# Sums made ahead for 49 pairs of weight chunks instead of 44 in a hybrid decoder layer

## The chip, the cores and the metric

One core of a Trainium2 chip runs the whole layer. The metric is the device time of one execution in microseconds. Engines are named as the profile names them: PE is TensorE's matmul, PEld its weight load, DVE is VectorE, ACT is ScalarE, POOL is GpSimd, SP the engine that issues most loads.

## The reference

```python
s = concat([meta_tokens, x])                       # 16 + 256 tokens, width 2048
s = s + 0.5 * swiglu(rms_norm(s), ffn1_w_gu, ffn1_w_down)     # inner width 5632
h = rms_norm(s); q, k, v, b, c, u = split(h @ w_in)
y_att, y_conv = diff_attention(q, k, v), b * short_conv(c * u)
s = s + sum(sigmoid(h @ w_gate) * (branches @ w_branch)) @ w_out
s = s + 0.5 * swiglu(rms_norm(s), ffn2_w_gu, ffn2_w_down)
out = rms_norm(s)[16:]
```

`swiglu(h, w_gu, w_down)` is `(silu(h @ gate) * (h @ up)) @ w_down`, where gate and up are the two halves of `w_gu`. All is float32.

## The kernel before

Every operand of a product is split into a high part, the value rounded to the short format that TensorE takes (a cast on ScalarE), and a low part, the rest (a subtraction on VectorE): `wh` and `wl` for weights. A product is three matmuls: high by high, low by high, high by low.

The change is in the second feed-forward network, whose gate and up stage has eleven units, 0 to 10, of 512 columns of gate and the same 512 of up. A unit runs over eight pairs of 128-row chunks of the weights. The activation (256 tokens) is the stationary operand, a weight tile the moving one, 512 columns wide. A pair is a 2 by 2 block matrix (two token blocks by two chunks) times a 2 by 2 block matrix (two chunks by gate and up). It is computed in one of three ways, a letter in the unit's plan:

- D: eight products, from two weight tiles of 1024 columns (`wh` and `wl` of one chunk's gate and up).
- S: seven products, from four tiles (512, 1024, 1024 and 1024 columns). Sums of weight blocks (`t13`, `t24`) are made by VectorE when the pair is reached, and sums of activation blocks (`sp`) are needed besides.
- P: seven products like S, but `t13` and `t24` were made in an earlier stage and are loaded from DRAM (`made`), while three instead of four blocks of the weights are loaded.

Each of eight accumulators (`pg1` to `pg7`, `pgx`) fills one PSUM bank. After the last pair VectorE evicts them (lines 692 to 703), ScalarE applies the silu, VectorE multiplies (line 716, `cup`), and in pair 1 of the next unit (the plan's second entry) TensorE transposes `cup` back (line 729, `mt_ps`), one half of it after each of the pair's first tiles.

Sums of the activation are made by `Mixed.combine`: four 128 by 128 sums, cast and subtracted into a tile `sp`. For the second network they are made for pairs 2, 3, 5, 6 and 7 and kept in the pool `a` for all eleven units. The activation `h3` is eight tiles, one per pair; tiles 4 to 7 lie in wide slots of 1280 columns of which they use 1024.

Making ahead is done by `Making`, during the first network: for each P pair and each half of its columns POOL loads four blocks (`mk`), VectorE adds in three instructions (lines 306 to 308), POOL stores (`made`). A step is due every five chunks of the first network's products (`tick`, `TICKS`). Its buffers are three of the pool `aux` and two of the tag `tt`; `aux` also takes the sums `sp` of the attention stage, made near the end of the first network.

A scheduler fixes the order of each engine's instructions when the program is built, from the order in which they are written and its own estimate of when things are ready; at run time each engine keeps that order. Pieces of work put into `side` are taken up one at a time, once a pair. Weight tiles have three buffers each for `wh` and `wl`, so a cast waits until TensorE has finished with the tile three back; loads run up to two pairs ahead, with four buffers `st`, and SP issues them in its order.

Of the kernel before, what the change touches and what calls it, by code (L numbers as in the profile page):

```python
# [9 lines left out]
F32 = mybir.dt.float32  # L10
# [5 lines left out]
P = 128  # L16
# [4 lines left out]
F = 5632  # L21
DC = D // P
GC = 4
GW = GC * P
# [12 lines left out]
PIECE = 320  # L37
# [10 lines left out]
B_PLAN = ("DDDSDSDS", (1, 2), {(2, 1): 3, (4, 1): 5, (6, 1): 7}, ())  # L48
FFN2_FIRST = ("DDDPDPPP", (1,), {}, ())
FFN2 = ("DDPPDSPP", (1,), {(4, 1): 5}, ())  # L50
OUT_FIRST = ("DDSDSDSD", (1,), {(1, 1): 2, (3, 1): 4, (5, 1): 6}, ())
OUT = ("DDDDSDSD", (), {(3, 1): 4, (5, 1): 6}, ())
DOWN_FIRST = ("DDDDDDSD", (1,), {(5, 1): 6}, ())
# [4 lines left out]
TICKS = 5  # L58
MAKE_AHEAD = 3
MAKE_BUFS = N_AUX + 2  # L60
MADE = [(u, p) for u in range(F // GW) for p, kind in enumerate((FFN2 if u else FFN2_FIRST)[0]) if kind == "P"]


@with_exitstack
def decoder_layer(ctx: ExitStack, tc: tile.TileContext, t, out):
    nc = tc.nc
# [52 lines left out]
    def load_vectors():  # L119
# [7 lines left out]
        out=mask[:, T - P :],  # L127
        in_=mask[:, T - P :],
# [25 lines left out]
    class Act:  # L154


        def __init__(self, name, chunks, width, wide_slots=(), piece=None):
            self.width, self.lead = width, 0 if piece is None else piece - width
            self.tiles = []
            for g in range(chunks // 2):  # L160
                if g in wide_slots:
                    w = piece or width
                    raw = apool.tile([P, 4 * PIECE], F32R, tag="big", bufs=N_BIG, name=f"{name}{g}")
                    self.tiles.append(raw[:, : 4 * w].rearrange("p (c l w) -> p c l w", c=2, l=2))
                else:
                    self.tiles.append(apool.tile([P, 2, 2, width], F32R, tag="act", name=f"{name}{g}"))

# [147 lines left out]

    for n, (u, p) in enumerate(MADE):
        spare.extend(Making(n, u, p, k) for k in range(2))
# [212 lines left out]
    class Mixed:  # L530
# [22 lines left out]
        def combine(self, p, f, pool=None):  # L553
            a11, a12, a21, a22 = (f[:, c, i * P : (i + 1) * P] for i in range(2) for c in range(2))
            q = tmp.tile([P, 4, P], F32, tag="sc", name="sums")
            nc.vector.tensor_sub(q[:, 0, :], a21, a22)
            nc.vector.tensor_sub(q[:, 1, :], q[:, 0, :], a11)
            nc.vector.tensor_sub(q[:, 2, :], a11, a21)
            nc.vector.tensor_add(q[:, 3, :], a12, q[:, 1, :])
            if pool is None:  # L560
                sp = (aux if self.in_aux else apool).tile([P, 4, 2, P], F32R, tag="act", name=f"sp{p}")
            else:
                sp = pool.tile([P, 4, 2, P], F32R, tag="norm", bufs=1, name=f"sp{p}")
            nc.scalar.copy(out=sp[:, :, 0, :], in_=q)
            nc.vector.tensor_sub(sp[:, :, 1, :], q, sp[:, :, 0, :].bitcast(F32))
            self.sums[p] = [[sp[:, k, lo, :] for lo in range(2)] for k in range(4)]
# [142 lines left out]
    def gate_up_mix(plan, a, rtok, w_gu, g, m, gi):  # L709


        def end(gt, up):
            for i in range(2):
                r = rtok[:, i : i + 1]
                nc.scalar.activation(gt[:, i, :], gt[:, i, :], AF.Silu, scale=r)
                nc.vector.scalar_tensor_tensor(
                    out=up[:, i, :], in0=up[:, i, :], scalar=r, in1=gt[:, i, :], op0=ALU.mult, op1=ALU.mult
                )
            for k in range(2):
                later.append(lambda k=k: back(m, 2 * gi + k, up, k))  # L720

        mixed(plan, a, w_gu[g], "pg", end, made[g])

    def back(act, g, mt, k):

        pt = bank("mt_ps")
        for c in range(2):
            for i in range(2):
                nc.tensor.transpose(
                    pt[:, (2 * c + i) * P : (2 * c + i + 1) * P], mt[:, i, (2 * k + c) * P : (2 * k + c + 1) * P], ident  # L730
                )
        tl, f = act.tiles[g], pt.rearrange("p (c t) -> p c t", c=2)
        nc.scalar.copy(out=tl[:, :, 0, :], in_=f)
        nc.vector.tensor_sub(tl[:, :, 1, :], f, tl[:, :, 0, :].bitcast(F32))
# [43 lines left out]
    for half in halves:  # L778
        m = gate_up(h1, half, t["ffn1_w_gu"], norm1, 0, before1 if half is halves[0] else None)
# [313 lines left out]
    h3 = Act("h3", DC, SEQ, range(4, NH))  # L1093
    hn = Mixed(h3, G_FFN2, False)
    rtok3 = const.tile([P, 2], F32, name="rtok3")
    nss = const.tile([P, 2, 4], F32, name="nss")

    def squares(i, u, q):
        sq = wide([P, GW], "nsq")
        nc.scalar.activation(  # L1100
            sq, sT[i][u][:, q * GW : (q + 1) * GW], AF.Square, accum_out=nss[:, i, 2 * u + q : 2 * u + q + 1]
        )
# [73 lines left out]
    def out_done(u):  # L1176
        def f():
            if u == 0:
                side.append(lambda: None)
                for p in (0, 2):  # L1180
                    side.append(lambda p=p: [turned(p), turned(p + 1), squares(0, 0, p // 2), squares(1, 0, p // 2)])
                side.append(lambda: [hn.sum_of_parts(2, tmp), hn.sum_of_parts(3)])
            else:
                side.extend(
                    (
                        lambda: [turned(4), squares(0, 1, 0), squares(1, 1, 0)],
                        lambda: [turned(5), hn.sum_of_parts(5)],
                        lambda: [turned(6), squares(0, 1, 1), hn.sum_of_parts(6)],
                        lambda: [turned(7), squares(1, 1, 1)],
                        lambda: hn.sum_of_parts(7),  # L1190
                        norm_tok,
                    )
                )

        return f

    side.extend([lambda: None] * 2)
    side.append(lambda: mo.sum_of_parts(6))
    add_mix(OUT_FIRST, mo, w_out, 0, 0, 1.0, "", out_done(0))
    add_mix(OUT, mo, w_out, 0, 1, 1.0, "", out_done(1))  # L1200
# [33 lines left out]
    w_gu, w_down, w_last = t["ffn2_w_gu"], t["ffn2_w_down"], t["ffn2_w_down_last"]  # L1234
    thirds = [list(range(0, 4)), list(range(4, 8)), list(range(8, ng))]
    for half in thirds:
        m = Act("m", len(half) * GC, SEQ, range(4))
        for gi, g in enumerate(half):
            gate_up_mix(FFN2 if g else FFN2_FIRST, hn, rtok3, w_gu, g, m, gi)
        final = half is thirds[-1]  # L1240
        if final:
            for q in range(2):
                nc.gpsimd.dma_start(
                    out=gfin[q],
                    in_=t["norm_final"][q * W2 : (q + 1) * W2].rearrange("(o d) -> o d", o=1).to_broadcast([P, W2]),
# [74 lines left out]
def _laid_out(np, inputs):  # L1320
# [8 lines left out]
    for name in ("ffn1_w_gu", "ffn1_w_down"):  # L1329
# [15 lines left out]
            np.stack([_quarter(w[2 * p * P : 2 * (p + 1) * P], u * GW + k * GW // 2, GW // 2) for k in range(2)])  # L1345
            for u, p in MADE
        ]
# [8 lines left out]
def _quarter(rows, c, n):  # L1356

    a, b = rows[:P], rows[P:]
    blocks = [a[:, c : c + n], a[:, F + c : F + c + n], b[:, F + c : F + c + n], b[:, c : c + n]]
    return _stacked(blocks)  # L1360
# [24 lines left out]
```

## Time and profile before

| | |
|---|---|
| median of 3 runs | 2138.35 us (2138.34 to 2138.82) |
| profiled execution | 2138.54 us, span 2136.3 us |
| PE busy | 2125.1 us, 99% of the span |
| DVE, ACT, POOL busy | 1709.7 us (80%), 1121.1 us (52%), 126.7 us (6%) |
| DMA | 533.04 MB, mean 250 GB/s |
| `mk` loads, `made` stores | 88 each, 512 KB |
| `t` loads from `made` | 88, 512 KB |

A row of a timeline gives the start in us from the span's start, the duration, the engine, the line, the operation, what it writes and reads, and in brackets the idle time of the engine before it with what ended it. Starts on one engine can lie closer than durations, since instructions overlap at their ends. In this execution the units' eight pairs begin at 1772.9 us for unit 6; units 0 to 3, 4 to 7 and 8 to 10 are each followed by their part of the product with `w_down`.

### The profile page before, as it was taken

To read this page: it belongs to the slowest core of one execution; us is meant where nothing else is said; L and a number is where in the kernel's file an instruction comes from. 1 tells how busy PE (TensorE), PEld (TensorE's weight loads), DVE (VectorE), ACT (ScalarE), POOL (GpSimd) and SP (SyncE) were. 2 spreads that over 40 slices of the span, in tenths; PEclk is the share of its full clock that TensorE was granted. 3 is DMA by queue.
4 is the path that set the end of the run, shared out by engine and by line. 5 is a ranking of instruction groups with operands and counts; after the bars stand their busy time and mean duration, and the time that the engine had idled before them with its cause. 6 is when DMAs were issued, how large, how long until landed. Compare 5 with 4: busy or idle time off the path is not lost.

```text
span 2136.3 us, 33292 instructions
## 1 busy us (share of the span) xinstructions
PE 2125.1 (99%) x13129; PEld 1919.3 (90%) x13129; DVE 1709.7 (80%) x2343; ACT 1121.1 (52%) x1414; POOL 126.7 (6%) x201
## 2 busy tenths in 40 slices
PE   9999999999999999999999999999999999999998
PEld 9999999999999998899998888888888888888887
DVE  7777676667776668867888888899999889988998
ACT  6444443344443455545545555557665566655665
POOL 0111111111111000000000000000000000000000
PEclk9999999999999999999999999999999999999999
DMA  8888988889898545543455555557875888768863
GB/s 302 319 314 318 330 320 315 318 317 329 298 338 314 189 178 187 188 158 140 158 184 191 197 197 196 208 207 251 275 281 202 276 281 290 247 220 298 293 217 138
DMA packets 98364, 533.04 MB, mean 250 GB/s; under 512 B 11680, under 2 KB 11936, under 8 KB 56224
## 3 DMA queue, kind: packets, MB, share of 16 engines
q1 hardware_dynamic: 69696, 432.72, 57.4%
q0 software_dynamic: 27936, 97.53, 13.1%
q8 instruction: 102, 1.67, 0.3%
q10 hardware_dynamic: 576, 0.67, 0.1%
q14 instruction: 54, 0.44, 0.1%
HBM read 478.45 MB, written 48.23 MB: 247 GB/s over the span
## 4 chain that ended last, share of the span: by engine, by line
PE 98%; DVE 1%; ACT 0%; DMA 0%; issue 0%; SPq 0%; DVEq 0%; ACTq 0%
PE pg L595 6%; PE pg L593 6%; PE pg L594 6%; PE pd L397 4%; PE pd L395 4%; PE pu L397 4%; PE pu L395 4%; PE pu L396 4%; PE pd L396 4%; PE pg L397 4%; PE pg L395 4%; PE pg L396 4%; PE pd L595 4%; PE pd L593 4%; PE pd L594 3%; PE g L595 2%
## 5 line engine op out<-in xcount | busy, mean ns | idle before, releaser
L384 DVE TENSOR_TENSOR wl<-st,wh 128x1024 fp32r<-128x1024 f32 (+1 forms) x329 | 400.8, 1220 | 253.2 <-ACT wh L379 253.0
L379 ACT CAST wh<-st 128x1024 fp32r<-128x1024 f32 (+1 forms) x328 | 343.4, 1048 | 484.3 <-PE pd L396 145.4
L499 DVE TENSOR_TENSOR wl<-st,wh 128x1024 fp32r<-128x1024 f32 (+1 forms) x424 | 463.5, 1105 | 55.7 <-ACT wh L498 50.7
L498 ACT CAST wh<-st 128x1024 fp32r<-128x1024 f32 (+1 forms) x424 | 396.5, 959 | 201.1 <-PE pdx L594 59.9
L498 ACT CAST wh<-t 128x1024 fp32r<-128x1024 f32 x182 | 189.5, 1052 | 219.6 <-DVE t L634 148.6
L499 DVE TENSOR_TENSOR wl<-t,wh 128x1024 fp32r<-128x1024 f32 x182 | 220.1, 1223 | 66.7 <-ACT wh L498 63.2
L395 PE MATMUL pg<-h,wh 128*128 128x272 f32 x704 | 201.9, 288 | 1.4 <-ACT h L211 1.4
L397 PE MATMUL pd<-mh,wl 128*128 128x272 f32 x704 | 203.3, 289 | 0.0
L395 PE MATMUL pd<-mh,wh 128*128 128x272 f32 x704 | 202.5, 288 | 0.0
L395 PE MATMUL pu<-h,wh 128*128 128x272 f32 x704 | 202.1, 287 | 0.0
L397 PE MATMUL pu<-h,wl 128*128 128x272 f32 x704 | 202.0, 287 | 0.0
L396 PE MATMUL pu<-h,wh 128*128 128x272 f32 x704 | 201.9, 287 | 0.0
L396 PE MATMUL pg<-h,wh 128*128 128x272 f32 x704 | 201.8, 288 | 0.0
L396 PE MATMUL pd<-ml,wh 128*128 128x272 f32 x704 | 200.9, 285 | 0.0
L397 PE MATMUL pg<-h,wl 128*128 128x272 f32 x704 | 200.2, 288 | 0.1
L593 PE MATMUL pg<-wh,h 128*128 128x512 f32 x366 | 143.5, 392 | 0.0
L594 PE MATMUL pg<-wh,h 128*128 128x512 f32 x366 | 142.8, 390 | 0.0
L595 PE MATMUL pg<-wl,h 128*128 128x512 f32 x366 | 142.4, 392 | 0.0
L395 PEld LDWEIGHTS pg<-h,wh 128*128 128x128 f32 x704 | 133.2, 190 | 1.7 <-ACT h L211 1.7
L396 PEld LDWEIGHTS pd<-ml,wh 128*128 128x128 f32 x704 | 133.6, 190 | 0.0
L396 PEld LDWEIGHTS pg<-h,wh 128*128 128x128 f32 x704 | 133.3, 190 | 0.0
L395 PEld LDWEIGHTS pu<-h,wh 128*128 128x128 f32 x704 | 132.8, 189 | 0.0
(383 smaller groups left out, 4984.2 us busy)
## 6 DMA issues: line engine op xcount, KB each, us to landing
st<-in_ffn_w_gu_dram SPq DMA_DIRECT2D x128, 1024.0 KB, 7.2
st<-in_ffn_w_down_dram SPq DMA_DIRECT2D x82, 1024.0 KB, 5.3
mk<-in_ffn_made_of_dram POOLq DMA_DIRECT2D x88, 512.0 KB, 8.5
made<-mk POOLq DMA_DIRECT2D x88, 512.0 KB, 7.0
t<-made SPq DMA_DIRECT2D x88, 512.0 KB, 5.6
st<-in_ffn_w_gu_dram SPq DMA_DIRECT2D x44, 768.0 KB, 5.8
st<-in_w_in_dram SPq DMA_DIRECT2D x32, 1024.0 KB, 4.8
st<-in_w_gate_dram SPq DMA_DIRECT2D x32, 1024.0 KB, 4.8
```

Of the source, the lines that this page charges most:

```text
L379: nc.scalar.copy(out=wh[:, :m, :], in_=sw)
L384: last_wl[:] = [nc.vector.tensor_sub(wl[:, :m, :], sw, wh[:, :m, :].bitcast(F32)).ins]
L395: nc.tensor.matmul(a, wh[:, i, f], act.part(c, 0, t0, t1), start=first, stop=False)
L396: nc.tensor.matmul(a, wh[:, i, f], act.part(c, 1, t0, t1), start=False, stop=False)
L397: nc.tensor.matmul(a, wl[:, i, f], act.part(c, 0, t0, t1), start=False, stop=last)
L498: part_last[:] = [nc.scalar.copy(out=wh, in_=src).ins]
L499: part_last.append(nc.vector.tensor_sub(wl, src, wh.bitcast(F32)).ins)
L593: nc.tensor.matmul(ps[k], hi, wh, start=first, stop=False)
L594: nc.tensor.matmul(ps[k], lo, wh, start=False, stop=False)
L595: nc.tensor.matmul(ps[k], hi, wl, start=False, stop=left[k] == 0)
```

## The change

Pair 1 of units 6 to 10 becomes a P pair. Its activation sums are made once, by one more entry of `side` in unit 0, and written not into a tile of a pool but into the unused 256 columns of the four wide tiles of `h3`, 128 of high part and 128 of low part in each. That makes their cast and subtraction four instructions of 128 columns each instead of one of 512. The number of P pairs goes from 44 to 49, and with it the halves that are made from 88 to 98.

```diff
+FFN2_MORE = ("DPPPDSPP", (1,), {(4, 1): 5}, ())
...
-MADE = [(u, p) for u in range(F // GW) for p, kind in enumerate((FFN2 if u else FFN2_FIRST)[0]) if kind == "P"]
+MORE_IN = (6, 7, 8, 9, 10)
+def _unit_plan(u):
+    return FFN2_MORE if u in MORE_IN else FFN2 if u else FFN2_FIRST
+MADE = [(u, p) for u in range(F // GW) for p, kind in enumerate(_unit_plan(u)[0]) if kind == "P"]
...
                     raw = apool.tile([P, 4 * PIECE], F32R, tag="big", bufs=N_BIG, name=f"{name}{g}")
                     self.tiles.append(raw[:, : 4 * w].rearrange("p (c l w) -> p c l w", c=2, l=2))
+                    self.rest.append(raw[:, 4 * w : 4 * PIECE])
...
             nc.vector.tensor_add(q[:, 3, :], a12, q[:, 1, :])
+            if pool is self.act:
+                self.sums[p] = []
+                for k in range(4):
+                    sp = self.act.rest[k][:, : 2 * P].rearrange("p (l t) -> p l t", l=2)
+                    nc.scalar.copy(out=sp[:, 0, :], in_=q[:, k, :])
+                    nc.vector.tensor_sub(sp[:, 1, :], q[:, k, :], sp[:, 0, :].bitcast(F32))
+                    self.sums[p].append([sp[:, lo, :] for lo in range(2)])
+                return
...
                         norm_tok,
+                        lambda: hn.sum_of_parts(1, h3),
...
-            gate_up_mix(FFN2 if g else FFN2_FIRST, hn, rtok3, w_gu, g, m, gi)
+            gate_up_mix(_unit_plan(g), hn, rtok3, w_gu, g, m, gi)
```

The rows below are the built program's order, with buffer numbers. Those of the changed kernel carry its own lines: L507 and L508 are the cast and the subtraction of lines 498 and 499 before, L709 to L720 the evictions of 692 to 703, L733 is 716, L746 is 729, and L573 and L574 are the new cast and subtraction.

VectorE between units 0 and 1, before. `st_15514` and `st_15516` are the weights of pairs 0 and 1 of unit 1.

```order
L499 TENSOR_TENSOR wl_15537<-st_15514,wh_15536 128x1024
L696 TENSOR_TENSOR cgate_15508<-pg4_15146,u2x_15401 128x512 [waits DVE_49]
L698 TENSOR_TENSOR cup_15507<-pg5_15340,u2x_15401 128x512
L702 TENSOR_TENSOR cgate_15508<-pg7_15344,cgate_15508 128x512 [waits DVE_49,PE_49]
L699 TENSOR_TENSOR cup_15507<-cup_15507,u2x_15401 128x512 [waits DVE_49]
L499 TENSOR_TENSOR wl_15552<-st_15516,wh_15551 128x1024 [waits DMAHW7_49,Activation_49]
L700 TENSOR_TENSOR cup_15507<-pg3_15142,cup_15507 128x512 [waits DVE_49,PE_49]
L703 TENSOR_TENSOR cup_15507<-cup_15507,pg7_15344 128x512
```

The same place now, from the second tile of pair 0 (`st_15594`) to the first of pair 1 (`st_15596`); ahead of it stand L559 (`mf`), L713 and three differences L565 to L567.

```order
L508 TENSOR_TENSOR wl_15617<-st_15594,wh_15616 128x1024
L568 TENSOR_TENSOR sums_15564<-mf_15562,sums_15564 128x128 [waits DVE_49]
L574 TENSOR_TENSOR h34_14402<-sums_15564,h34_14402 128x128 [waits Activation_49]
L574 TENSOR_TENSOR h35_14403<-sums_15564,h35_14403 128x128 [waits Activation_49]
L574 TENSOR_TENSOR h36_14404<-sums_15564,h36_14404 128x128 [waits Activation_49]
L715 TENSOR_TENSOR cup_15587<-pg5_15405,u2x_15466 128x512
L574 TENSOR_TENSOR h37_14405<-sums_15564,h37_14405 128x128 [waits Activation_49]
L716 TENSOR_TENSOR cup_15587<-cup_15587,u2x_15466 128x512 [waits DVE_49]
L719 TENSOR_TENSOR cgate_15588<-pg7_15409,cgate_15588 128x512
L717 TENSOR_TENSOR cup_15587<-pg3_15207,cup_15587 128x512 [waits DVE_49]
L720 TENSOR_TENSOR cup_15587<-cup_15587,pg7_15409 128x512
L508 TENSOR_TENSOR wl_15632<-st_15596,wh_15631 128x1024 [waits DMAHW7_49]
```

All evictions now stand ahead of pair 1's first `wl`, and four low parts among them.

ScalarE at that place, before: after the casts of pair 1 come those of pair 2 (`st_15530`), the small one first.

```order
L498 CAST wh_15577<-st_15516 128x1024 [waits DVE_49,PE_49]
L498 CAST wh_15597<-st_15530 128x512 [waits DMAHW5_49,DVE_49]
L715 ACTIVATE cgate_15508<-cgate_15508,rtok3_14341 128x512 [waits DVE_49]
L498 CAST wh_15603<-st_15530 128x1024 [waits PE_49]
L498 CAST wh_15626<-t24_15533 128x1024 [waits DMAHW1_49,DVE_49,PE_49]
```

And now, where pair 2's weights are `st_15610`.

```order
L507 CAST wh_15657<-st_15596 128x1024 [waits DVE_49,PE_49]
L573 CAST h34_14402<-sums_15564 128x128 [waits DVE_49]
L573 CAST h35_14403<-sums_15564 128x128 [waits DVE_49]
L573 CAST h36_14404<-sums_15564 128x128
L507 CAST wh_15683<-st_15610 128x1024 [waits DVE_49,DMAHW5_49,PE_49,Activation_49]
L573 CAST h37_14405<-sums_15564 128x128 [waits DVE_49]
L507 CAST wh_15677<-st_15610 128x512 [waits Activation_49]
```

The 1024 cast of pair 2, which waits for its load (`DMAHW5`), stands between the third and the fourth of the new casts.

TensorE in pair 1 of unit 6, before, from the last product of its first tile.

```order
L593 MATMUL pgx_18020<-wh_18004,h31_14334 128x512
L594 MATMUL pgx_18020<-wh_18004,h31_14334 128x512
L595 MATMUL pgx_18020<-wl_18005,h31_14334 128x512
L729 MATMUL mt_ps_18072<-ident_75,cup_17960 128x128 [waits DVE_49]
L593 MATMUL pg2_18008<-wh_18030,h31_14334 128x512 [waits Activation_49]
```

The same now, from the pair's first matmul; `wh_18088`, `wh_18098` and `wh_18118` are pair 1's first three tiles, `wh_18166` is the first of pair 2.

```order
L610 MATMUL pg3_18106<-wh_18088,h37_14405 128x512 [waits Activation_49]
L611 MATMUL pg3_18106<-wh_18088,h37_14405 128x512
L612 MATMUL pg3_18106<-wl_18089,h37_14405 128x512 [waits DVE_49]
L610 MATMUL pg2_18102<-wh_18098,h31_14399 128x512 [waits Activation_49]
L611 MATMUL pg2_18102<-wh_18098,h31_14399 128x512
L610 MATMUL pg4_18110<-wh_18118,h31_14399 128x512 [waits Activation_49]
L612 MATMUL pg2_18102<-wl_18099,h31_14399 128x512 [waits DVE_49]
L611 MATMUL pg4_18110<-wh_18118,h31_14399 128x512
L610 MATMUL pg3_18106<-wh_18166,sp2_15005 128x512 [waits Activation_49]
L611 MATMUL pg3_18106<-wh_18166,sp2_15005 128x512
L612 MATMUL pg4_18110<-wl_18119,h31_14399 128x512 [waits DVE_49]
L746 MATMUL mt_ps_18145<-ident_75,cup_18040 128x128 [waits DVE_49]
```

The first transpose came after the pair's first twelve matmuls and comes after eleven now, and four of these belong to tiles that were cast later before.

VectorE there, before and now; `st_17969` and `st_18049` are pair 1's weights, `t24_18052` its loaded sums, L716 and L733 what the transpose needs.

```order
L499 TENSOR_TENSOR wl_18005<-st_17969,wh_18004 128x1024 [waits DMAHW6_49,Activation_49]
L700 TENSOR_TENSOR cup_17960<-pg3_17655,cup_17960 128x512 [waits DVE_49]
L703 TENSOR_TENSOR cup_17960<-cup_17960,pg7_17786 128x512
L499 TENSOR_TENSOR wl_18031<-st_17969,wh_18030 128x1024 [waits PE_49,Activation_49]
L716 SCALAR_TENSOR_TENSOR cup_17960<-cup_17960,rtok3_14341,cgate_17961 128x512 [waits DVE_49]
```

```order
L508 TENSOR_TENSOR wl_18089<-st_18049,wh_18088 128x512 [waits DMAHW6_49,Activation_49]
L717 TENSOR_TENSOR cup_18040<-pg3_17735,cup_18040 128x512 [waits DVE_49]
L720 TENSOR_TENSOR cup_18040<-cup_18040,pg7_17866 128x512
L508 TENSOR_TENSOR wl_18099<-st_18049,wh_18098 128x1024 [waits Activation_49]
L508 TENSOR_TENSOR wl_18119<-t24_18052,wh_18118 128x1024 [waits DMAHW2_49,PE_49,Activation_49]
L733 SCALAR_TENSOR_TENSOR cup_18040<-cup_18040,rtok3_14406,cgate_18041 128x512 [waits DVE_49]
```

One more subtraction of 1024 columns stands ahead of the product that the transpose needs, and the first one is half as wide.

More of the change, by code (lines that the diff above doesn't have):

```diff
@@ L158, in __init__ @@
             self.width, self.lead = width, 0 if piece is None else piece - width
-            self.tiles = []
+            self.tiles, self.rest = [], []
             for g in range(chunks // 2):
```

## Prediction

> **What bounds the kernel now.** I read the busy shares and the chain of waits first, then the stretches of one gate and up unit, then the timelines of the engines at the places the change touches.
>
> ```profile
> PE 2125.1 (99%) x13129; PEld 1919.3 (90%) x13129; DVE 1709.7 (80%) x2343; ACT 1121.1 (52%) x1414; POOL 126.7 (6%) x201
> ...
> PE 98%; DVE 1%; ACT 0%; DMA 0%; issue 0%; SPq 0%; DVEq 0%; ACTq 0%
> ```
>
> TensorE carries the end: 98% of the chain. A matmul removed anywhere shortens the kernel, and a wait of TensorE added anywhere lengthens it; there is no idle time later that would take it back. How close the others follow is read from unit 6, one of the five changed, and from the stretch that loads most (columns: stretch, length, busy time and count of PE, PEld, DVE, ACT, POOL, then granted clock, DMA share, GB/s).
>
> ```profile
> 1772.90:1814.00 41.10, 41.10 (x187) 34.00 (x186) 37.54 (x43) 27.52 (x32) 0.00 (x0) 1.00 0.82 281
> 1907.50:1948.00 40.50, 40.50 (x180) 33.57 (x179) 34.13 (x37) 21.56 (x23) 4.59 (x6) 1.00 0.90 305
> ```
>
> TensorE is busy in all of both; VectorE has 3.56 us left of a unit's 41.1, ScalarE 13.6.
>
> **The saving.** An eight-product pair is two tiles of four products of three matmuls, 24; a seven-product pair is 21. Five pairs: 15 matmuls fewer. Their price is the distance of starts in a full queue, not the 0.39 us shown, which overlap:
>
> ```profile
> 1772.92 0.39 PE L593 MATMUL pg<-wh,h 128*128 128x512 f32 x1
> ...
> 1778.36 0.39 PE L593 MATMUL pg<-wh,h 128*128 128x512 f32 x1
> ...
> 1780.85 0.39 PE L595 MATMUL pgx<-wl,h 128*128 128x512 f32 x1
> 1781.08 0.27 PE L729 MATMUL mt_ps<-ident,cup 128*128 128x128 f32 x1
> ```
>
> These are the first matmuls of pairs 0 and 1 of unit 6: 24 matmuls in 5.44 us, 0.227 each. So 3 x 0.227 = 0.68 us a unit, 3.4 us in all, 0.16%, is the most this can bring: "faster by over 0.2%" (4.3 us, about what a measurement of this kernel tells from no change) is out of reach. The Trainium skill (TensorE: Matmul & The Clock Gate, "Back-to-back issue gap") gives about 131 ns as the sustained spacing at 512 columns; by it 15 matmuls would be an estimated 2.0 us and the sum below 1.4 us higher. The trace disagrees, with 227 ns.
>
> **What the pair costs the other engines.** Two subtractions of 1024 columns become one of 512 and three of 1024:
>
> ```profile
> 1776.35 1.22 DVE L499 TENSOR_TENSOR wl<-st,wh 128x1024 fp32r<-128x1024 f32 x1
> 1777.49 0.68 DVE L700 TENSOR_TENSOR cup<-pg,cup 128x512 f32<-128x512 f32 x1
> 1778.09 0.68 DVE L703 TENSOR_TENSOR cup<-cup,pg 128x512 f32<-128x512 f32 x1
> 1778.68 1.22 DVE L499 TENSOR_TENSOR wl<-st,wh 128x1024 fp32r<-128x1024 f32 x1
> 1779.82 1.41 DVE L716 SCALAR_TENSOR_TENSOR cup<-cup,rtok,cgate 128x512 f32<-128x512 f32 x2
> 1781.15 1.81 DVE L499 TENSOR_TENSOR wl<-st,wh 128x512 fp32r<-128x512 f32 x2
> ...
> 1785.34 1.23 DVE L499 TENSOR_TENSOR wl<-t,wh 128x1024 fp32r<-128x1024 f32 x1 [0.65 <-ACT wh L498]
> ```
>
> By starts, a 1024 costs 1.13 us, a 512 0.60. Net +1.73 us a unit; with 0.68 us less to hide it, 3.56 - 2.41 = 1.15 us stays idle: VectorE does not become the bound over a unit. Its idle time ahead of `wl` ends by ScalarE's casts, which wait for a weight buffer from TensorE, so it runs ahead until buffers stop it. ScalarE gets one 512 and one 1024 cast more, about 1.6 us of its 13.6. DMA: 768 KB less load but two stored tiles more, net +0.79 MB on 281 GB/s x 41.1 us = 11.55 MB, so 12.3 MB in 40.4 us, 305 GB/s: the second stretch above moved just that with TensorE fully busy. Cost nothing; the cover is TensorE's 40 us and two pairs of prefetch.
>
> Averages hide one place, pair 1 itself: it stands where VectorE has the evictions of the unit before behind it. By the order now written, VectorE does from 1776.35: 512 (0.60), L700, L703 (0.60 each), 1024, 1024 (1.13 each), so the first L716 starts at 1780.41, 0.59 later than before, and ends 0.70 later (half of the 1.41 and the overlap), at 1781.1. TensorE's order has 11 matmuls of pairs 1 and 2 ahead of the first transpose of `cup`: 1778.36 + 11 x 0.227 = 1780.86. It waits about 0.3 us for L716. Continued the same way, the next tight places (the cast of pair 2's 1024 tile, which needs pair 1's buffer; the PSUM banks of products 5 and 7, which the two transposed tiles free) come out with 0.1 to 0.2 us to spare. I take a wait of 0.3 us: -0.4 net in each of units 6, 7, 9 and 10; ends -0.7 (no wait) and +0.3 (each of three tight places misses by 0.2 more). Unit 8 has no transposes in pair 1, and VectorE waits for buffers there: -0.7 (to -0.4). Together -2.3, ends -3.4 and +0.8.
>
> **The sixth sum, unit 0 to 1.** Its VectorE work is one 512 (0.60), four 128-column differences and four 128-column lower parts, its ScalarE work four 128-column casts. All of it is placed among unit 0's evictions:
>
> ```profile
> 1476.34 0.29 DVE L556 TENSOR_TENSOR sums<-mf 128x128 f32<-128x128 f32 x1
> 1476.54 0.29 DVE L558 TENSOR_TENSOR sums<-mf 128x128 f32<-128x128 f32 x1
> ...
> 1484.69 1.22 DVE L499 TENSOR_TENSOR wl<-st,wh 128x1024 fp32r<-128x1024 f32 x1
> 1485.83 0.69 DVE L696 TENSOR_TENSOR cgate<-pg,u2x 128x512 f32<-128x512 f32 x1
> 1486.43 0.68 DVE L698 TENSOR_TENSOR cup<-pg,u2x 128x512 f32<-128x512 f32 x1
> ...
> 1488.22 1.22 DVE L499 TENSOR_TENSOR wl<-st,wh 128x1024 fp32r<-128x1024 f32 x1
> ```
>
> ```profile
> 1485.96 1.06 ACT L498 CAST wh<-st 128x1024 fp32r<-128x1024 f32 x1 [0.44 <-PE pgx L594]
> 1489.69 0.62 ACT L498 CAST wh<-st 128x512 fp32r<-128x512 f32 x1 [2.67 <-DMA st<-in_ffn_w_gu_dram]
> ```
>
> ```profile
> 1488.71 0.39 PE L593 MATMUL pg<-wh,h 128*128 128x512 f32 x1
> ...
> 1490.07 0.84 PE L595 MATMUL pg<-wl,h 128*128 128x512 f32 x3
> ```
>
> Small ones cost 0.20 each. VectorE now, from 1484.69: 512, L696, three differences (to 1486.5), pair 0's `wl` (to 1487.6: TensorE needs it at 1485.99 + 8 x 0.227 = 1487.8, in time), a difference, three lower parts, L698 (to 1489.0), and then the fourth lower part, which needs the fourth cast. ScalarE reaches the casts after the row of 1485.96, at 1487.0, does three by 1487.6, and then stands at the 1024 cast of pair 2, ordered between the third and the fourth: that waits for the load which in the row above lands at 1489.7. So the cast of 0.95 us, then the fourth, done at 1490.9. VectorE waits for it, queued behind it are the lower part, L699, L702, L700, L703 (0.20 + 4 x 0.60) and only then pair 1's `wl`, 1493.5 to 1494.7. TensorE starts pair 1 at 1488.71, its order now has all eight `wh` matmuls first (to 1490.5), and waits for `wl`: 4.2 us. The next load is issued when pair 0's `wl` frees its buffer, 1.8 us later than before, so for that long two loads share the DMA engines instead of three and the load in question may land sooner, by at most half of it, 0.9 (an estimate): I take 3.9. Ends 2.4 (the load does not hold the fourth cast) and 4.3; below the first only if the queue's order is not kept.
>
> **The makings.** Ten more halves are made in the first network:
>
> ```profile
> L306 DVE TENSOR_TENSOR mk<-mk x88: 679/684/687, 49.3 to 695.5; 128x512 f32<-128x512 f32 x88
> L314 POOL DMA_DIRECT2D made<-mk x88: 711/728/740, 51.2 to 697.6; - x88
> ...
> DMA to landing us min/median/max: 3.4/7.5/12.1
> ```
>
> ```profile
> 769.14 1.22 DVE L384 TENSOR_TENSOR wl<-st,wh 128x1024 fp32r<-128x1024 f32 x1
> ...
> 771.83 1.23 DVE L384 TENSOR_TENSOR wl<-st,wh 128x1024 fp32r<-128x1024 f32 x1 [0.87 <-ACT wh L379]
> 774.79 1.23 DVE L384 TENSOR_TENSOR wl<-st,wh 128x1024 fp32r<-128x1024 f32 x1 [1.74 <-ACT wh L379]
> ```
>
> One comes every five chunks, two chunks every 2.97 us: 7.4 us, so the last adds fall at 695.5 + 10 x 7.4 = 770. Nine lie in VectorE's idle 1.7 us of every 2.97. The tenth shares its buffers with the attention sums: its fetch waits for a store two makings older, and by a landing of about 7 us each way its data is due within a us of its add; `wl` behind it may be late, and the idle time of the next row takes it back. 0.2 us, ends 0 and 2.
>
> **Sum**: -2.3 + 3.9 + 0.2 = +1.8 on the profiled execution's 2138.54 (span 2136.3 and 2.2 around it). That execution is 0.2 above the median of the runs, 2138.35; against the median 2140.2. All ends low: -3.4 + 2.4 + 0 = -1.0; all high: 0.8 + 4.3 + 2 = +7.1; they do not fall together, so its own range is 2138.0 to 2142.4.
>
> **Rivals.**
> A: the saving alone counts, since the wait in unit 1 stays under 1 us: that needs the fourth cast to find its data without the 1024 cast's load ahead of it and TensorE to have work beside `wl`. For it: in the two stretches above TensorE never stops, with the same engines behind it. Against: the row with 2.67 us of waiting for just this load. -3.4 to -1.5: 2135.0 to 2136.9.
> B, the other side: the granted clock falls in the wait.
>
> ```profile
> 2125.00:2130.00 5.00, 3.04 (x26) 2.84 (x24) 3.17 (x10) 1.55 (x7) 0.00 (x0) 1.00 0.48 197
> 2130.00:2136.00 6.00, 0.00 (x0) 0.00 (x0) 1.27 (x5) 1.33 (x2) 0.00 (x0) 0.74 0.49 175
> ```
>
> TensorE's last matmul ends about 2128.0; a mean of 0.74 over the last 6 us means full speed for 2.9 of them and half after, so the clock halved some 4.8 us after the work ended. A wait of 3.9 us is close to that. Halved for as long again as the wait, it would cost 2 us, for twice as long 4: 2142.2 to 2144.2; it decides once the wait passes the time the gate looks back. The Trainium skill (TensorE: Matmul & The Clock Gate, "What's actually happening") says the clock halves after an idle window of about 3.4 us that runs freely, and returns after a busy one; the trace's 4.8 us agrees with it (between one window and two), and no run here shows a wait in between.
> C: the tight places of units 6 to 10 all miss, and each transition costs 1 us instead of saving: five times +1.1 over my value, 2143 to 2146. For it: margins of 0.1 to 0.2 us; against: what TensorE loses there the other engines gain as lead.
>
> **How the numbers follow.** My sum 0.70, A 0.12, B 0.08, C 0.08, the rest (the change without any effect) 0.02. Slower by over 0.2% (past 2142.6): most of C, half of B, little of mine, 0.13. Faster by over 0.2% 0.01. Within 0.86. The range reaches to A's upper end and past my own, 2136.6 to 2142.8, leaving out the rest of A and the upper parts of B and C.
>
> **What would show it.** In the profile after: 15 matmuls fewer; one idle stretch of TensorE of 3 to 4.3 us near 1491 with `wl` of L508 as its releaser, a VectorE wait for ScalarE's cast of L573 just before, and a ScalarE wait for the load before that; units 6, 7, 9 and 10 about 40.7 us long instead of 41.1, each with a wait of 0.3 us at the first transpose; unit 8 0.7 us shorter and without one; no TensorE idle time near 770; the clock at 1.00 after 1495. Wrong it would be if the wait near 1491 is absent or twice as long, or if TensorE stops elsewhere.

## The result, and the profile after

The changed kernel takes 2143.68 us (median of 14 runs, 2142.01 to 2145.17), the kernel before 2138.68 us (14 runs, 2138.34 to 2139.56): 1.0023 times as long, 95% interval 1.0016 to 1.003. It is slower by 5.0 us, more than the 4.3 us called measurable ahead, and lies above the range of 2136.6 to 2142.8. The profiled execution took 2143.95 us with a span of 2142.1, against 2138.54 and 2136.3.

The page of the changed kernel, busy shares and chain of waits:

```profile
PE 2125.4 (99%) x13114; PEld 1916.1 (89%) x13114; DVE 1732.7 (81%) x2392; ACT 1127.5 (53%) x1428; POOL 139.3 (7%) x221
...
PE 96%; DMA 1%; DVE 1%; ACT 1%; issue 1%; SPq 0%; DVEq 0%; ACTq 0%
```

The 15 matmuls are gone, and yet TensorE is busy 0.3 us longer. Neither the shares nor the chain tell why: the 2% that the chain moved from TensorE to others are some 40 us, among them two loads of 8 and 10 us that ran while TensorE worked, and the kernel with the sum alone (below), with the same long wait, shows 98%. The place is seen in TensorE's own timeline, in the transition from unit 0 to unit 1:

```profile
1490.02 0.39 PE L611 MATMUL pgx<-wh,h 128*128 128x512 f32 x1
1494.74 1.65 PE L612 MATMUL pg<-wl,h 128*128 128x512 f32 x3 [4.33 <-DVE wl L508]
1496.18 0.63 PE L612 MATMUL pgx<-wl,h 128*128 128x512 f32 x1
1496.61 0.63 PE L610 MATMUL pg<-wh,h 128*128 128x512 f32 x1
```

There are two things in it. TensorE starts nothing for 4.71 us, 4.48 more than the 0.23 that usually lie between two starts. And behind the wait a matmul takes 0.63 us instead of 0.39, and the next starts 0.43 us later instead of 0.23. Four stretches of 3.41 us at that place (PE's busy time first, the granted clock third from the end):

```profile
1489.73:1493.14 3.41, 0.68 (x4) 0.22 (x2) 2.28 (x5) 2.34 (x4) 0.00 (x0) 1.00 0.61 248
1493.14:1496.55 3.41, 1.81 (x4) 1.49 (x5) 3.41 (x5) 1.04 (x1) 0.00 (x0) 0.50 0.03 12
1496.55:1499.97 3.42, 3.42 (x10) 2.47 (x9) 2.33 (x3) 0.00 (x0) 0.00 (x0) 0.50 0.90 307
1499.97:1503.38 3.41, 3.41 (x20) 2.89 (x19) 2.25 (x3) 2.58 (x4) 0.00 (x0) 1.00 0.72 231
```

The clock is granted at half for exactly the second and third. From 1494.74, when work resumes, to 1499.97 that is 5.23 us at half speed: 2.6 us lost, if nothing else would have held TensorE up in that time.

Who made TensorE wait is read from VectorE's and then from ScalarE's timeline:

```profile
1488.05 0.70 DVE L715 TENSOR_TENSOR cup<-pg,u2x 128x512 f32<-128x512 f32 x1
1490.86 0.29 DVE L574 TENSOR_TENSOR h<-sums,h 128x128 fp32r<-128x128 f32 x1 [2.11 <-ACT h L573]
...
1493.46 2.36 DVE L508 TENSOR_TENSOR wl<-st,wh 128x1024 fp32r<-128x1024 f32 x2
```

```profile
1486.62 0.69 ACT L573 CAST h<-sums 128x128 fp32r<-128x128 f32 x3
1489.58 1.05 ACT L507 CAST wh<-st 128x1024 fp32r<-128x1024 f32 x1 [2.27 <-DMA st<-in_ffn_w_gu_dram]
1490.54 0.29 ACT L573 CAST h<-sums 128x128 fp32r<-128x128 f32 x1
```

A load releases a 1024 cast at 1489.58, the fourth 128-column cast of the sixth sum stands behind that, a 128-column lower part on VectorE behind the cast, four evictions behind the lower part, and `wl` behind those.

Where the rest went, from the starts of the stages in TensorE's timeline (before, after, difference):

| stretch | before | after | difference |
|---|---|---|---|
| up to the second network | 1439.43 | 1439.08 | -0.35 |
| units 0 to 3 | 167.04 | 174.22 | +7.18 |
| first down projection | 85.26 | 85.27 | 0.01 |
| units 4 to 7 | 163.32 | 162.89 | -0.43 |
| second down projection | 85.27 | 85.27 | 0 |
| units 8 to 10 | 122.25 | 121.61 | -0.64 |
| from there to the last matmul | 65.19 | 65.14 | -0.05 |

The +7.18 is 4.48 of wait, 2.6 of half clock and 0.1 not followed up. Units 6 to 10 bring 1.07 us of their 3.4. What holds them up, first a transpose of unit 6 and then pair 3 of unit 8:

```profile
1788.10 0.33 PE L746 MATMUL mt_ps<-ident,cup 128*128 128x128 f32 x1 [0.16 <-DVE cup L733]
...
1964.54 0.50 PE L612 MATMUL pg<-wl,sp 128*128 128x512 f32 x1 [0.19 <-DVE wl L508]
```

Both waits are short in the brackets, since the profile models the end of a matmul; from start to start they cost 0.34 (1787.53 to 1788.10) and 0.35 us (1963.96 to 1964.54) more than the usual 0.23. The first is L733, as forecast. The second goes back through `wl` and ScalarE's cast to a load of sums made ahead:

```profile
1962.17 2.00 ACT L507 CAST wh<-t 128x1024 fp32r<-128x1024 f32 x2 [2.18 <-DMA t<-made]
```

### The profile page after: what moved, and what is told of

Read it like the earlier page. It is cut to its first block, busy times and chain, and to the rows that moved or that the text cites. A ratio compares the mean times of both kernels' runs of the same rounds, so it can differ in the third digit from the quotient of the medians.

```text
span 2142.1 us, 33400 instructions
## 1 busy us (share of the span) xinstructions
PE 2125.4 (99%) x13114; PEld 1916.1 (89%) x13114; DVE 1732.7 (81%) x2392; ACT 1127.5 (53%) x1428; POOL 139.3 (7%) x221
## 4 chain that ended last, share of the span: by engine, by line
PE 96%; DMA 1%; DVE 1%; ACT 1%; issue 1%; SPq 0%; DVEq 0%; ACTq 0%
PE pg L612 6%; PE pg L610 6%; PE pg L611 6%; PE pd L406 4%; PE pd L404 4%; PE pu L405 4%; PE pu L404 4%; PE pu L406 4%; PE pd L405 4%; PE pg L406 4%; PE pg L405 4%; PE pg L404 4%; PE pd L612 4%; PE pd L610 3%; PE pd L611 3%; PE g L612 2%
## 5 line engine op out<-in xcount | busy, mean ns | idle before, releaser
L508 DVE TENSOR_TENSOR wl<-st,wh 128x1024 fp32r<-128x1024 f32 (+1 forms) x424 | 460.9, 1100 | 50.3 <-ACT wh L507 45.3
L507 ACT CAST wh<-st 128x1024 fp32r<-128x1024 f32 (+1 forms) x424 | 392.8, 953 | 194.4 <-PE pdx L611 59.4
L507 ACT CAST wh<-t 128x1024 fp32r<-128x1024 f32 x192 | 199.7, 1053 | 221.9 <-DVE t L651 150.8
L508 DVE TENSOR_TENSOR wl<-t,wh 128x1024 fp32r<-128x1024 f32 x192 | 231.5, 1223 | 63.3 <-ACT wh L507 60.0
L610 PE MATMUL pg<-wh,h 128*128 128x512 f32 x371 | 145.9, 395 | 0.0
L611 PE MATMUL pg<-wh,h 128*128 128x512 f32 x371 | 145.5, 392 | 0.0
L404 PEld LDWEIGHTS pg<-h,wh 128*128 128x128 f32 x704 | 132.5, 189 | 2.4 <-ACT h L220 1.7
L404 PEld LDWEIGHTS pu<-h,wh 128*128 128x128 f32 x704 | 132.8, 189 | 0.0
L405 PEld LDWEIGHTS pu<-h,wh 128*128 128x128 f32 x704 | 132.7, 189 | 0.0
```

The costliest lines, as they stand in the source:

```text
L404: nc.tensor.matmul(a, wh[:, i, f], act.part(c, 0, t0, t1), start=first, stop=False)
L405: nc.tensor.matmul(a, wh[:, i, f], act.part(c, 1, t0, t1), start=False, stop=False)
L507: part_last[:] = [nc.scalar.copy(out=wh, in_=src).ins]
L508: part_last.append(nc.vector.tensor_sub(wl, src, wh.bitcast(F32)).ins)
L610: nc.tensor.matmul(ps[k], hi, wh, start=first, stop=False)
L611: nc.tensor.matmul(ps[k], lo, wh, start=False, stop=False)
```

## The experiments

Theory 1 is that the sixth sum makes one wait of 4.5 us through the load that its fourth cast stands behind, that this wait halves the clock, and that both together are more than the saving. Its rivals: the wait alone counts (theory 2), or units 6 to 10 and the makings cost it (theory 3). All times below are medians, each with the kernel before measured in the same series; a difference to the changed kernel is that between the two distances to the kernel before.

**The sum alone.** `MORE_IN = ()`, all else as changed.

> The kernel before with the sixth sum alone: it is made where the changed kernel makes it, but no unit uses it and no further halves are made. Theory 1 (the sixth sum costs it all: the 4.5 us in which TensorE stands near 1490, and some 2.4 us at half the granted clock behind it): 2138.7 + 4.5 + 2.4 = 2145.6 us, 2144.5 to 2147. Theory 2 (the wait counts, the clock costs nothing): 2143.2. Theory 3 (the loss of the changed kernel lies in units 6 to 10 or in the makings): 2138.7 to 2140.

2145.24 us against 2138.49 (1.0033, 1.0021 to 1.0046). Slower than the changed kernel, without one of its changed units: theory 3 falls. The wait and the half clock stand in its trace:

```profile
1495.27 1.02 PE L612 MATMUL pg<-wl,h 128*128 128x512 f32 x2 [4.18 <-DVE wl L508]
```

```profile
1495.00:1502.00 7.00, 6.73 (x27) 5.33 (x28) 5.67 (x8) 2.54 (x3) 0.00 (x0) 0.76 0.64 206
```

A mean of 0.76 over 7 us is half clock for 3.4 us, one window where the changed kernel's trace has two.

**The sum in the middle of unit 1.**

```diff
+                        *[lambda: None] * 4,
                         lambda: hn.sum_of_parts(1, h3),
```

> The changed kernel, with four empty entries ahead of the sixth sum in the list of side work, so that it is made in the middle of unit 1, behind the evictions of unit 0, and its four lower parts no longer stand ahead of a waited-for wl with a load between. Theory 1: the wait near 1490 and the half clock go, and what is left is the saving of 3.4 us less some 1.9 us of short waits in units 6 to 10: 2143.7 - 4.5 - 2.4 = 2136.8, 2135.8 to 2138, TensorE at full clock throughout. Theory 3 (units 6 to 10 or the makings cost it): 2141 to 2143.5.

2138.05 us against 2138.49 (0.9999, 0.999 to 1.0008): 5.4 us below the changed kernel, by the place of the sum alone. The stretch where the wait was:

```profile
1490.00:1495.00 5.00, 5.00 (x28) 4.13 (x27) 4.81 (x7) 3.26 (x5) 0.00 (x0) 1.00 0.81 306
1495.00:1502.00 7.00, 7.00 (x33) 5.76 (x32) 7.00 (x9) 5.19 (x7) 0.00 (x0) 1.00 0.77 252
```

The time is 1.2 us above the 2136.8 expected, at the edge of the range. Its trace has a new wait of 0.66 us at 1511.7, where unit 1's chain of three sums for its S pair (L649 to L651) now comes late, and 0.7 us of unit 8's wait for the load, twice that of the changed kernel's trace.

**Casts on VectorE.** One line of `combine`:

```diff
-                    nc.scalar.copy(out=sp[:, 0, :], in_=q[:, k, :])
+                    nc.vector.tensor_copy(out=sp[:, 0, :], in_=q[:, k, :])
```

> The changed kernel with the four 128-column casts of the sixth sum on VectorE instead of ScalarE: 0.8 us more for VectorE, but no step of it stands behind the 1024 cast that waits for its load. Theory 1 in its first step (the long wait comes from the fourth cast standing behind that load): TensorE waits about 1.3 us for the wl of pair 0 and 0.7 us for that of pair 1, in two pieces too short for the clock: 2143.7 - (4.5 - 2.0) - 2.4 = 2138.8, 2138 to 2140.5. Rival (VectorE's own 2.2 us of work ahead of wl make the wait, whoever casts): one wait of 4 us or more and half clock behind it, 2143 to 2145.

2138.87 us against 2138.49 (1.0002, 0.9994 to 1.0011). The sum stays in its place and gives VectorE more work, and 4.6 us of the 5.0 are gone; TensorE waits in two pieces, 1.27 and 0.28 us, the clock stays at 1.00:

```profile
1488.43 0.96 PE L612 MATMUL pg<-wl,h 128*128 128x512 f32 x3 [1.11 <-DVE wl L508]
```

So the long wait came by way of ScalarE and its load and not from the amount of VectorE's work.

**The wait filled.** Products of zeros keep TensorE at work in the wait: three of them, and in a second kernel four (`fill` holds that number in the first tile of pair 1 of unit 1, and is empty everywhere else).

```diff
-            nc.tensor.matmul(ps[k], lo, wh, start=False, stop=False)
+            mm = nc.tensor.matmul(ps[k], lo, wh, start=False, stop=False)
+            if fill and k == "x":
+                with tc.issue_after(mm.ins):
+                    for _ in range(fill.pop()):
+                        nc.tensor.matmul(ps[k], mask[:, :P], sT[0][0][:, :GW], start=False, stop=False)
```

> The changed kernel with three products of zeros (128x512, f32) added into the bank of the last product, between the eight wh matmuls of pair 1 of unit 1 and its wl matmuls: TensorE works through most of the same wait, and the wait for wl stays. Theory 1: the granted clock stays 1.00 behind the wait, 2143.7 - 2.4 = 2141.3, 2140.5 to 2142, and the runs lie as close together as those of the kernel before (within 1.3 us instead of 3.2). Theory 2 (the clock costs nothing): 2143.7.

2141.72 us (1.0016, 1.0007 to 1.0025), near the 2141.3, but the runs spread from 2139.94 to 2144.32, and the profiled one has a halved window all the same: the products end 2.0 us before `wl` comes. Hence the fourth:

> As the one with three products of zeros in the wait, with four: 3.4 us of work in the wait of 4.5, which leaves TensorE idle for 1.1 to 1.3 us, 30 to 40% of a window of 3.41 us at most, where the waits of ten lengths had no halving up to 58%. The three products left 2.0 us and one halved window in the profiled run. Theory (the clock is a cost of its own, and it comes from the idle share of a window): no halved window, 2143.7 - 2.4 = 2141.3, 2140.8 to 2141.8, and the runs lie within 1.5 us of each other instead of 3.2 and 4.4. Rival (the spread and the cost come from something else at this place): 2142 to 2144 with a spread of 3 us.

No halved window and a spread of 1.6 us, but 2143.03 us (1.0021, 1.0012 to 1.003): 0.5 below the changed kernel and not 2.4, and within the rival's range. Its trace shows waits in the place of the clock: 0.54 us at the transposes of unit 1, which TensorE now reaches ahead of VectorE, and 1.2 us in unit 8 for the load of made tiles, where the changed kernel's trace has 0.35. To keep unit 8 out of it, the same four products in the kernel with the sum alone:

> The kernel before with the sixth sum alone (2145.24 us, one halved window in its trace), and four products of zeros in the wait. Theory (the halved windows cost 1.7 to 2.6 us of their own, of which up to 0.5 comes back as a wait at the transposes, since TensorE reaches them sooner): 2145.2 - 1.2 to 2.1 = 2143.1 to 2144.0, no halved window. Rival (the clock costs next to nothing, since TensorE would wait for VectorE behind the wait anyway): 2144.8 or above.

2143.96 us against the 2145.24 without them. The wait is there, the clock is not halved, and the wait at the transposes follows:

```profile
1494.71 0.98 PE L618 MATMUL pg<-wl,h 128*128 128x512 f32 x3 [0.86 <-DVE wl L508]
...
1496.50 0.33 PE L753 MATMUL mt_ps<-ident,cup 128*128 128x128 f32 x1 [0.35 <-DVE cup L740]
```

```profile
1495.00:1502.00 7.00, 6.65 (x33) 5.01 (x33) 6.85 (x9) 3.51 (x5) 0.00 (x0) 1.00 0.73 241
```

So the half clock is a cost of its own, 1.3 us here by the medians. These come from two series, and the intervals against the kernel before overlap, but the runs hardly do: 2145.14 to 2146.24 without the products, 2143.86 to 2145.16 with them. In the traces, where the wait ends at the same distance from the start of the stage, units 0 to 3 take 173.31 us without and 172.34 with them, 1.0 less: 1.7 for one halved window, less 0.5 that TensorE then waits at the transposes, and 0.2 not followed up.

For the changed kernel, with two halved windows in its trace, the same stretch takes 174.22 us, and 172.53 with four products: 1.7 less. That the whole time fell by 0.5 alone is in part unit 8, whose stage took 122.53 us in that execution instead of 121.61. So the share of the clock in the changed kernel's loss is about 1.7 us by the traces of one execution each, net of what TensorE would have waited anyway.

**How long a wait halves the clock.** The kernel before has three to twelve multiplications by 1.0 added behind the evictions of units 0 to 9, 0.45 us each, and the `wl` of the next pair 1 is ordered behind them. A second kernel has the same numbers in another order.

```diff
+                for _ in range(HELD.pop(0) if HELD and made else 0):
+                    last = nc.vector.tensor_scalar_mul(up[:, 1, :], up[:, 1, :], 1.0)
+                hold_wl[:] = [last.ins]
```

> The kernel before with waits put in: after the evictions of units 0 to 9 VectorE multiplies the finished tile by 1.0 in place three, four, ... twelve times, and the wl of pair 1 of what comes next is ordered behind that, so TensorE waits there, a little longer each time, from about 1 to 5 us by an estimate of 0.3 to 0.6 us for each multiplication. What it tells: how long a wait must be for the granted clock to halve. Theory W1 (only a wait that fills a whole window of 3.4 us): no halving below 3.4 us, each time above 6.8. Theory W2 (a window that is mostly idle is enough, wherever its edges fall): waits of about 2 us or more halve it in part of the cases, and each halving lasts 3.4 us or a multiple of that.

> The kernel before with the same ten numbers of multiplications in another order (12, 5, 10, 7, 4, 11, 6, 9, 8, 3), so that waits of each length fall elsewhere in the windows of 3.41 us. Theory (a window that is idle for about 60% or more halves the clock for the next one; a window under 20% idle brings it back): waits under 2 us do nothing, waits of 2.1 to 3.4 us halve it where they lie within one window, waits above 4.2 us always, each for 3.41 or 6.83 us.

2174.48 and 2171.32 us in one run each. In both traces the beginnings of the halved stretches lie whole multiples of 3.41 us apart, so each wait can be cut at these edges. From the first kernel: a wait of 1.85 us, one of 2.32, and one of 4.16:

```profile
1744.09:1747.50 3.41, 1.72 (x9) 1.12 (x8) 3.27 (x7) 0.18 (x1) 0.00 (x0) 1.00 0.03 14
1747.50:1750.92 3.42, 3.42 (x17) 2.82 (x17) 3.42 (x5) 1.46 (x2) 0.00 (x0) 1.00 0.48 132
1788.46:1791.88 3.42, 1.26 (x6) 0.86 (x5) 3.35 (x6) 1.00 (x1) 0.00 (x0) 1.00 0.00 0
1791.88:1795.29 3.41, 3.41 (x11) 2.71 (x10) 2.65 (x5) 0.63 (x2) 0.00 (x0) 0.50 0.70 209
...
2058.12:2061.53 3.41, 0.50 (x3) 0.07 (x1) 3.17 (x9) 0.00 (x0) 0.00 (x0) 1.00 0.00 0
2061.53:2064.94 3.41, 2.32 (x7) 1.69 (x8) 3.41 (x5) 1.04 (x1) 0.00 (x0) 0.50 0.25 34
2064.94:2068.36 3.42, 3.42 (x10) 2.74 (x9) 2.89 (x4) 0.59 (x1) 0.00 (x0) 0.50 0.82 334
```

From the second kernel, a wait of 3.1 us (from 1889.3 to 1892.4) that an edge cuts in two:

```profile
1887.22:1890.63 3.41, 2.14 (x11) 1.54 (x9) 3.17 (x8) 1.02 (x1) 0.00 (x0) 1.00 0.06 26
1890.63:1894.04 3.41, 1.61 (x7) 1.35 (x8) 3.38 (x5) 1.05 (x1) 0.00 (x0) 1.00 0.00 0
1894.04:1897.46 3.42, 3.42 (x20) 2.80 (x19) 3.38 (x5) 1.51 (x2) 0.00 (x0) 1.00 0.87 295
```

2.3 us inside one window halve the clock, 3.1 us over two do not; nor does the second kernel's own wait of 2.3 us, which an edge cuts at 2020.34. In these two kernels every window at full clock in which TensorE was busy for 1.31 us or less was followed by half clock, and none with 1.61 or more; W1 falls, W2 holds. A halved window with 2.75 us of work (2013.74 in the first kernel) was followed by another, one with 3.27 us (1884.04) by full clock. The one window that does not fit is that of the three products of zeros, 1.62 us busy and halved, at the border.

**The makings alone.** 98 halves made, units as before, no sixth sum.

> The kernel before with the makings of the changed one: 98 halves are made in the first network and stored, ten of them for nothing, no sixth sum, and every unit keeps its old pairs. Theory (they lie in VectorE's idle time, and the start of the second gate and up stage comes some 0.35 us sooner in the traces of all kernels that have them): 2138.5 - 0.35 to 2138.5. Rival (they take some 0.2 to 2 us from TensorE, as the prediction bounded it): 2138.7 to 2140.5.

2137.81 us against 2138.7 (0.9996, 0.9987 to 1.0005): they cost nothing, and the time is 0.9 less, below the range of theory and rival. 0.28 us of this is seen in the output projection at 1375, where a wait for `wl` of 0.44 us before is 0.16 now. Another 0.4 lies outside the span: every execution of a kernel that stores 94 or 98 halves took 1.7 to 1.9 us more than its span, and those that store 88 took 2.2 to 2.3 (once 3.0). Why ten more stores in the first network shorten either was not found.

**Other places for the sum, other units.** First into unit 2, then there with the transposes of the changed units one tile later:

```diff
-            if p in turn_at and later:
+            if p in turn_at and later and (kinds[p] == "D" or n):
```

> The changed kernel with the sixth sum in the middle of unit 2 (eleven empty entries ahead of it), behind the transposed tiles of that unit, where VectorE has idle time, and two lower parts ahead of the sums of the S pair, since in unit 1 the sum pushed that pair's chain of sums late (TensorE waited 0.66 us there). Theory: that wait goes, 2138.05 - 0.66 = 2137.4, 2136.8 to 2138. Rival (VectorE is as short of time in unit 2 as in unit 1, so the sum costs its 0.7 us wherever it stands): 2138.0 or above.

> As the one with the sum in unit 2, and in units 6, 7, 9 and 10 the transposes come one tile later: behind the second and third tile of pair 1, and no longer behind its first and second, three matmuls (0.68 us) later. Theory (the wait of 0.35 us at the first transpose for L733, and 0.14 us in which transposes stand apart): four times 0.35 to 0.5 less, 2137.4 - 1.4 to 2.0 = 2135.4 to 2136.0. Rival (the banks that the transposed tiles need, or the casts of m behind them, come late instead): no gain, 2137.4 or above.

2138.17 and 2137.62 us against 2138.7. Both miss, and both lie in the rival's range. In unit 2 the sum still costs 0.3 us at its S pair, at 1553. With the later transposes their wait is gone (in its place 0.24 us beside them), but the first `wl` of the down projection behind unit 7 comes 0.62 us late and unit 8 waits 0.7: what TensorE had waited for at the transposes it waits for further on.

Then the sum at the end of the first down projection, with the five units as changed:

> The changed kernel with the sixth sum made at the end of the first down projection after units 0 to 3, where VectorE has 2.3 us of idle time in the trace of before; units 6 to 10 as changed. Theory (the sum costs nothing there, and of the saving of 3.4 us the units give back 2.7: four times 0.36 + 0.14 at the transposes, and 0.7 in unit 8): the 2137.8 of the kernel with the makings alone, less 0.7: 2137.1, 2136.5 to 2137.7. Rival (the units give back all of it): 2137.8 or above. Rival (they give back little, and the sum was what cost): 2134.5 to 2136.

2137.12 us against 2138.57 (0.9994, 0.9985 to 1.0002), as expected, with no wait at the sum and, in the profiled execution, none in unit 8. From there two choices of units:

> As the one with the sum in the first down projection, with three units changed (5, 6 and 9) instead of five, all of them units with a transposed tile in pair 1 and with another gate and up unit behind them, and with the transposes one tile later. Nine matmuls fewer, 2.04 us. Theory (what gives the saving back are unit 8, whose load comes late, and the down projection behind unit 7, so without them most of it is kept, 0.45 to 0.6 a unit): 2137.8 - 1.4 to 1.8 = 2136.0 to 2136.4. Rival (VectorE gives it back wherever it is): 2137.4 to 2138.

2137.03 us (0.9993, 0.9984 to 1.0002), a miss, between theory and rival: no wait is left in its changed units, but units 5 and 6 save 0.80 us of 1.36 together, and nearly all of the rest is 0.24 us a unit of wider spacing at a weight tile behind the transposes.

> The kernel with the sixth sum in the first down projection, with units 5, 6, 7, 9 and 10 changed instead of 6 to 10. Theory (in unit 8 nothing holds TensorE up in pair 1, so the made tiles of pair 3, whose buffer comes free with pair 1, are wanted before they land; in unit 5 the transposes give them that time): no wait for a load of made tiles in the trace, the runs within 1.5 us of each other, 2136.6 to 2137.1. Rival (three seven-product pairs in a row wait for that load in any unit): the wait shows in unit 5, and the time stays at 2137.1 or above.

2137.00 us against 2138.61 (0.9993, 0.9984 to 1.0001), runs from 2136.55 to 2137.79, all of them below every run of the kernel before in that series (2138.35 to 2139.03). The wait for made tiles is gone with unit 8. These last three are the best versions: some 1.5 us below the kernel before, at the edge of what the interval can tell, and 6.6 below the changed kernel. The saved matmuls are not all of these 1.5 us: 0.4 is the time outside the span, the spans are 1.1 shorter (medians of 2135.2 and 2135.3 against 2136.3), and the makings alone had already brought 0.9.

## Why the prediction was wrong

- **The step that failed is the sum's treatment of the clock.** Half clock behind the wait in unit 1 stood as rival B at 0.08 and with nothing in the sum; it happened, in the trace for 5.23 us of work, 2.6 us, of which 1.7 came off when the wait was filled. The prediction read a tail of 4.8 us as the time to halving and called a wait of 3.9 "close to that". The inserted waits show that a window of 3.41 us need only be idle for some 60%. A wait of 4.2 us or more, of which one window always holds at least 2.1, should then halve the clock every time, and one of 3.9, as forecast, would miss only where an edge cuts it into two parts that are both under 2.1, in about one case of ten (an estimate from these windows). What depends on the phase is mostly one window or two. B should have been the likeliest case. Its 2142.2 to 2144.2 hold the result, in part by luck: the longer wait and the units' smaller saving, which B does not price, are in that time too.
- **The wait was mis-sized by 0.6 us**, 4.48 for 3.9 and above its upper end of 4.3. The chain behind it (load, 1024 cast, fourth cast, lower part, four evictions, `wl`) came as written. The allowance that failed is that of the load landing up to 0.9 us sooner with two loads in flight: it released the cast at 1489.58, 0.1 sooner than before, and `wl` came at 1493.46, as the prediction has it without the allowance, while TensorE, as the whole stage, ran some 0.3 us sooner.
- **Units 6, 7, 9 and 10** were forecast at -0.4 each. The wait at the transposes was right, 0.34 to 0.37 for 0.3; some 0.12 a unit of wider spacing beside it was not in the sum, and units 6 and 7 brought 0.43 together.
- **Unit 8** was forecast at -0.7 without a wait. With three seven-product pairs in a row, the third one's load of made tiles is issued when the first has freed its buffer, 5.1 us into the unit, here and in six other kernels (1951.87 in the changed one). It landed 10.2 us later, against a median of 5.6 for such loads, and TensorE waited 0.35 us; where it took 9.4 us there was no wait, where it took 11.1 one of 1.2. The cost of the loads was set to nothing because the mean GB/s fitted, and this is one load's buffer and landing. Why it lands so late was not followed up. (The prediction's "768 KB less load" is a slip: three blocks of 256 KB instead of four are 256 KB less. Its net of 0.79 MB is right.)
- **The makings** were right: their last adds start at 771 to 774 us (770 forecast), TensorE does not stop there, and their cost is nothing.
- Put together by the trace: 4.48 + 2.6 - 1.07 - 0.35, and 0.1 in the rest, is 5.7 where the sum had 1.8. The run's own time rose by 5.4, since the time outside the span fell by 0.4. Rival C gave a time near the result by a mechanism that is not in the trace.

## What to carry to other kernels

A small instruction placed on an engine's queue costs what stands ahead of it: a sum with four casts of 0.2 us cost 6.7 us, because one cast stood behind another that waited for a load, and with the casts on another engine, or the sum half a unit later, the kernel was 4.6 and 5.4 us faster. Where TensorE is the bound and waits over 2 us, price the clock with the wait: here, by the traces of one execution each, 1.0 us for one halved window and 1.7 for two, net of what it would have waited anyway. And when a change saves matmuls on an engine that others follow closely, expect most of it back as short waits further on: of 3.4 us the best versions kept 0.6 to 0.7 against the kernel with the makings alone.

## What the hardware showed that was not expected

- The clock is decided in windows of 3.41 us at fixed places in time: 2.3 us of waiting within one window halved it, 3.1 us across two did not. The Trainium skill (TensorE: Matmul & The Clock Gate, "What's actually happening") gives the window as 3413 ns and free-running, with which these traces agree; it speaks of an idle window, where here one idle for 61% was enough, and of a busy one for the return, where here one with 81% of work was not enough and one with 96% was.
- The runs of the changed kernel spread over 3.2 us, and the spread goes with the clock: the seven runs with a mean granted clock of 0.997 took 2143.95 to 2145.17 us, the seven with 0.998 took 2142.01 to 2143.41. One halved window is 0.0008 of a run's mean clock, so this fits two halved windows (as in the profiled run, of the first group) and one; how many each run had was not recorded. A wide spread by itself is no sign of such a wait: the kernel with the sum alone has the wait and spread over 1.1 us in five runs, the one with the sum in the first down projection has none and spread over 3.2, by one run of eleven.
- The same load of made tiles in unit 8, issued 5.1 us into the unit each time, landed after 9.4 to 11.1 us and cost 0 to 1.2 us in kernels that differ only far ahead of it, so a wait for a transfer that is just in time cannot be told from one profile.
